# State-space outputs of a hybrid diffusion layer, channel-major: two heads side by side in the array's columns, decays as broadcast rows

## The chip, the cores and the metric

The kernel runs on one core of one Trainium2 chip, in one launch. The metric is device time in microseconds (us). A core has a matrix engine (TensorE, PE in the profile, with its weight loads as PEld), a vector engine (DVE), a scalar engine (ACT), GpSimd (POOL) and SyncE (SP), which issues the DMAs here. SBUF is the on-chip memory of 128 partitions; PSUM holds the results of matmuls.

## The reference, cut to what matters

One layer over 512 latent tokens (and 256 context tokens) of 1024 channels: a modulated norm, one input projection, two token mixers (a state-space scan, "SSD", in both directions, and windowed attention), an output projection, then a gated feed-forward net. The change concerns the outputs of the scan. There are 32 heads of 64 channels in 4 groups of 8; each group has one B and one C of 128 state dimensions; tokens go in chunks of 128.

```python
def ssd_scan(xs, la, bm, cm, h0, with_output):
    ...
    cs = jnp.cumsum(ac, axis=-1)
    ...
    cb = jnp.einsum('bclgn,bcsgn->bgcls', cc, bc)
    scores = cb[:, :, None] * jnp.exp(segsum(ac))
    y_diag = jnp.einsum('bgrcls,bcsgrp->bclgrp', scores, xc)
    y_off = jnp.einsum('bclgn,bcgrpn,bgrcl->bclgrp', cc, states[:, :-1], jnp.exp(cs))
    return (y_diag + y_off).reshape(Bsz, L, G, R, P).astype(xs.dtype), final

def ssd_output(y, xs, z, d_skip, g):
    Bsz, L = y.shape[:2]
    y = y + d_skip.reshape(SSD_GROUPS, SSD_HPG, 1).astype(y.dtype) * xs
    return rmsnorm(y.reshape(Bsz, L, D_SSD) * jax.nn.silu(z), g)
```

The scan runs forward and backward, with its own step sizes dt and decays for each direction, and the two outputs are added. Since x is scaled by dt, the token's own term (l = s) appears in both directions.

## The kernel before, in words

All arithmetic is fp32. The large projections split each operand into a high and a low part and use three matmuls (lines L187, L188, L190; `gemm`), 512 tokens moving, 128 channels at a time. Weights are loaded by SP into `wraw` (3 buffers), split by ACT into `whi` (L144) and by DVE into `wlo` (L145).

After attention, one program list runs the four groups of the scan, with the projections of the next group placed between their steps (in the last group, gate projections `g_step` in their place). A scheduler then sets the order on each engine; every engine, and SP's queue of DMAs, works strictly in its order. `dt_tables` works out dt and the cumulated decays `cs`, writes `cs` to memory (`cs_d`), and `dt_turn` turns the tables token-major: `TA` (biases for the decays), `TB` (exp(cs) of both directions and dt) and `TC`.

For group g:

- `x_fn` projects four tiles of 128 channels, runs the short convolution and silu (L737 to L746) into a scratch tile `tc`, and `turn` transposes it on the PE (L765), so that `xs` is token-major.
- `states` makes the backward states of all chunks and the first forward state (L837, L855; the POOL scales the old state in L839, the DVE adds in L840).
- `chunk_in(c)` fetches `fb`, the decay rows of eight heads copied to all 128 partitions, one tile of 512 KB for each direction (L890, 4 buffers); makes B·C for the chunk (`cb`, L894); takes the diagonal of `cb` with a DVE reduction against the identity (L897) and forms `coef` = dt_b·diagonal + skip weight (L901); and makes `E`, the decayed scores of 4 heads, twice (L909 to L915).
- `chunk_out(c)` makes C·state for both directions (L924, C stationary, 512 columns of state moving), scales each by exp(cs) (DVE, L927), makes the diagonal part head by head (L931: E stationary, 64 columns of `xs` moving), adds `coef`·xs and both off-diagonal parts on the POOL (L936 to L938) and the whole into `y` (DVE, L939), token-major. Then `advance` makes the next forward state.
- `gate` turns `y` back to channel-major with 16 PE transposes (L953), multiplies it by the gate `zs`, fetched from memory (L950, L955), writes it to memory (`yz_d`, L956) and sums its squares (ACT L961, POOL L962).

The sum of squares `ssq` is read by the PE in `rms_sums` (L229), which stands among the first products of the next stage (`os_step`, which reads `yz_d` back through `y_split`, L1000 to L1003).

Of the kernel before, what the change touches and what calls it, by code (L numbers as in the profile page):

```python
# [9 lines left out]
F32 = mybir.dt.float32  # L10
# [8 lines left out]
P = 128  # L19
# [25 lines left out]
def tile_hybrid_layer(  # L45
# [62 lines left out]
    def misb():  # L108
        return bank("mis")
# [104 lines left out]
    ao_d = dpool.tile([8, P, L], F32, name="ao_d")  # L214
    yz_d = dpool.tile([16, P, L], F32, name="yz_d")
    cs_d = dpool.tile([64, L], F32, name="cs_d")
    tt_d = dpool.tile([64, 4], F32, name="tt_d")

    def col(base, i):
# [401 lines left out]
    TB = tabp.tile([P, 4, P], F32, name="TB")  # L621
    TC = tabp.tile([P, 4, 64], F32, name="TC")
    eT = tabp.tile([P, 64, 4], F32, name="eT")
    epool = ExitStack()
# [5 lines left out]
    def dt_tables(w):  # L630
# [61 lines left out]
        F["dt"] = sa, sb  # L692
        dump("dt", dt)
        dump("cs", cs)

    def dt_turn():
        sa, sb = F["dt"]
# [71 lines left out]
    def proj_steps(g):  # L769
        d = GR[g]  # L770

        def b_fn(w):
            d["xs"] = bp.tile([P, 4, 512], F32, tag="xs", name="xs", bufs=2)
            d["xsc"] = bp.tile([P, 2, 512], F32, tag="xsc", name="xsc", bufs=1)
            d["Bkc"] = bp.tile([P, 2, P], F32, tag="Bkc", name="Bkc", bufs=2)
# [19 lines left out]
        def x_fn(ct, w):  # L795
            i = 4 * g + ct
            pl, pc = accb(), accb()
            gemm([LAT(pl)], w)
            turn()
            gemm([CTX(pc)], w)  # L800
            for pp, n, dst in ((pl, L, d["xs"]), (pc, LC, d["xsc"])):
                xl = tmp("tc")
# [16 lines left out]
    def ssd_steps(g):  # L819
# [25 lines left out]
        def states():  # L845
# [35 lines left out]
            d["y"] = bp.tile([P, 4, 512], F32, tag="y", name="y", bufs=1)  # L881

        def chunk_in(c):
            fb = []
            for dr in range(2):
                f = bp.tile([P, 8, P], F32, tag="fb", name="fb", bufs=4)
                a = bass.AP(
                    tensor=cs_d.tensor, offset=cs_d.offset + (32 * dr + 8 * g) * L + c * P, ap=[[0, P], [L, 8], [1, P]]
                )
# [5 lines left out]
            cbd = bp.tile([P, 1], F32, tag="cbd", name="cbd", bufs=2)  # L895
            junk = bp.tile([P, P], F32, tag="junk", name="junk", bufs=1)
            V.tensor_tensor_reduce(  # L897
                junk, cb[:, :P], ident, op0=ALU.mult, op1=ALU.add, scale=1.0, scalar=0.0, accum_out=cbd
            )
            coef = bp.tile([P, 8], F32, tag="coef", name="coef", bufs=2)  # L900
            V.scalar_tensor_tensor(coef, TB[:, c, 96 + 8 * g : 104 + 8 * g], cbd, bcs[:, 8 * g : 8 * g + 8], ALU.mult, ALU.add)  # L901
            d["E"], d["coef"] = [], coef
            for q in range(2):
                E = bp.tile([P, 4, P], F32, tag="E", name="E", bufs=3)
                eb = misb()
# [10 lines left out]
                d["E"].append(E)  # L916

        def chunk_out(c):
            xs, y, coef = d["xs"], d["y"], d["coef"]
            tok = slice(c * P, (c + 1) * P)  # L920
            parts = []
            for dr, s in ((0, d["Sf"]), (1, d["Sb"][c])):
                ps = misb()
                T.matmul(ps, d["CT"][:, tok], s, start=True, stop=True)  # L924
                z0 = 32 * dr + 8 * g
                t = tmp("te")
                V.tensor_tensor(h8(t), h8(ps), bc64(TB[:, c, z0 : z0 + 8]), ALU.mult)  # L927
                parts.append(t)
            yd = misb()
            for h in range(8):  # L930
                T.matmul(  # L931
                    yd[:, h * 64 : (h + 1) * 64], d["E"][h // 4][:, h % 4, :], xs[:, c, h * 64 : (h + 1) * 64],
                    start=True, stop=True,
                )
            dx = bp.tile([P, 512], F32, tag="tf", name="dx", bufs=1)
            G.tensor_tensor(h8(dx), h8(xs[:, c, :]), bc64(coef), ALU.mult)  # L936
            G.tensor_tensor(dx, dx, parts[1], ALU.add)
            G.tensor_tensor(dx, dx, parts[0], ALU.add)  # L938
            V.tensor_tensor(y[:, c, :], yd, dx, ALU.add)  # L939
            if c < 3:  # L940
                d["Sf"] = advance(d["Sf"], 0, c, weigh_in(0, c))

        def gate():
            y = d["y"]
            if g == 0:
                dump("y", y[:, 1, :])
            for ct in range(4):
                i = 4 * g + ct
                zt = bp.tile([P, L], F32, tag="zs", name="zs", bufs=2)
                nc.sync.dma_start(zt, zs_d[i])  # L950
                ps = misb()
                for c in range(4):
                    T.transpose(ps[:, c * P : (c + 1) * P], y[:, c, ct * P : (ct + 1) * P], ident)  # L953
                yz = bp.tile([P, 512], F32, tag="tg", name="yz", bufs=2)
                V.tensor_tensor(yz, ps, zt, ALU.mult)  # L955
                nc.sync.dma_start(yz_d[i], yz)  # L956
                if i == 0:
                    S.activation(ssq, yz, AF.Square)
                else:
                    sq = bp.tile([P, 512], F32, tag="th", name="sq", bufs=1)  # L960
                    S.activation(sq, yz, AF.Square)  # L961
                    G.tensor_tensor(ssq, ssq, sq, ALU.add)  # L962

        r = [([], states)]
        for c in range(4):
# [406 lines left out]
```

## Time and profile before

| | us |
|---|---|
| median of 3 runs | 1318.2 (1317.3 to 1318.23) |
| the profiled execution | 1317.22 |
| its span | 1315.4 |
| PE busy / weight loads busy | 1270.1 / 1028.7 |
| DVE / ACT / POOL busy | 912.7 / 640.5 / 133.3 |

The span is what the profile covers of the execution; 1.8 us lie around it. The four groups of the scan lie between about 466 and 792 us. Matmuls are pipelined, so one matmul's duration overlaps the next one's; the time between starts, or a merged row of many, tells what one costs the PE. An fp32 matmul that is not split by hand appears as two records (x2).

### The profile page before, as it was taken

To read this page: it belongs to the slowest core of one execution; us is meant where nothing else is said; L and a number is where in the kernel's file an instruction comes from. 1 tells how busy PE (TensorE), PEld (TensorE's weight loads), DVE (VectorE), ACT (ScalarE), POOL (GpSimd) and SP (SyncE) were. 2 spreads that over 40 slices of the span, in tenths; PEclk is the share of its full clock that TensorE was granted. 3 is DMA by queue.
4 is the path that set the end of the run, shared out by engine and by line. 5 is a ranking of instruction groups with operands and counts; after the bars stand their busy time and mean duration, and the time that the engine had idled before them with its cause. 6 is when DMAs were issued, how large, how long until landed. Compare 5 with 4: busy or idle time off the path is not lost.

```text
span 1315.4 us, 17187 instructions
## 1 busy us (share of the span) xinstructions
PE 1270.1 (97%) x6434; PEld 1028.7 (78%) x6434; DVE 912.7 (69%) x1457; ACT 640.5 (49%) x1182; POOL 133.3 (10%) x104
## 2 busy tenths in 40 slices
PE   4989999999999999999999999999999999999996
PEld 2777777787778878778787787888888888888886
DVE  4578887888666588888888756776677767773333
ACT  4376666666535456475574654223444444442221
POOL 0000000000000024333443430000000000000000
PEclk8998999999999999999999999999999999999998
DMA  7612222211236235444455658767133433333331
GB/s 287 234 33 80 73 80 65 79 67 57 88 112 186 95 93 135 158 112 129 145 123 190 168 166 280 248 204 249 41 116 115 131 104 114 117 110 93 99 89 65
DMA packets 86931, 168.65 MB, mean 128 GB/s; under 512 B 6784, under 2 KB 42112, under 8 KB 86848
## 3 DMA queue, kind: packets, MB, share of 16 engines
q1 hardware_dynamic: 86848, 167.56, 40.9%
q8 instruction: 50, 0.82, 0.3%
q14 instruction: 33, 0.27, 0.1%
HBM read 150.62 MB, written 16.91 MB: 127 GB/s over the span
## 4 chain that ended last, share of the span: by engine, by line
PE 87%; DVE 6%; ACT 3%; issue 1%; DMA 1%; SPq 0%; POOL 0%; DVEq 0%; ACTq 0%; POOLq 0%
PE acc L187 21%; PE acc L188 21%; PE acc L190 21%; PE score L560 2%; PE pt L584 2%; PE mis L924 2%; PE mis L931 2%; PE mis L837 2%; PE po L589 2%; DVE wlo L145 1%; PE po L590 1%; PE mis L855 1%; ACT ta L485 1%; PE mis L765 1%; PE acc L332 1%
## 5 line engine op out<-in xcount | busy, mean ns | idle before, releaser
L145 DVE TENSOR_TENSOR wlo<-wraw,whi 128x1024 fp32r<-128x1024 f32 (+1 forms) x163 | 206.1, 1265 | 133.7 <-ACT whi L144 131.5
L144 ACT CAST whi<-wraw 128x1024 fp32r<-128x1024 f32 (+1 forms) x163 | 168.9, 1037 | 230.5 <-PE acc L188 199.2
L187 PE MATMUL acc<-hlh,whi 128*128 128x512 f32 (+1 forms) x512 | 212.0, 414 | 0.4 <-ACT whi L144 0.4
L190 PE MATMUL acc<-hlh,wlo 128*128 128x512 f32 (+1 forms) x512 | 203.3, 397 | 2.2 <-DVE wlo L145 2.2
L188 PE MATMUL acc<-hll,whi 128*128 128x512 f32 (+1 forms) x512 | 203.5, 398 | 0.0
L187 PE MATMUL acc<-mh,whi 128*128 128x512 f32 x384 | 149.6, 390 | 0.0
L190 PE MATMUL acc<-mh,wlo 128*128 128x512 f32 x384 | 149.4, 389 | 0.0
L188 PE MATMUL acc<-ml,whi 128*128 128x512 f32 x384 | 149.4, 389 | 0.0
L187 PEld LDWEIGHTS acc<-hlh,whi 128*128 128x128 f32 (+1 forms) x512 | 96.7, 189 | 22.1 <-issue 4.1
L190 PEld LDWEIGHTS acc<-hlh,wlo 128*128 128x128 f32 (+1 forms) x512 | 96.3, 188 | 22.1 <-DVE wlo L145 2.9
L188 PEld LDWEIGHTS acc<-hll,whi 128*128 128x128 f32 (+1 forms) x512 | 96.7, 189 | 20.4 <-issue 4.1
L190 PEld LDWEIGHTS acc<-mh,wlo 128*128 128x128 f32 x384 | 72.1, 188 | 15.1
L187 PEld LDWEIGHTS acc<-mh,whi 128*128 128x128 f32 x384 | 72.1, 188 | 15.0
L188 PEld LDWEIGHTS acc<-ml,whi 128*128 128x128 f32 x384 | 72.1, 188 | 14.7
L839 POOL TENSOR_TENSOR st<-st,eT 128x512 f32<-128x512 f32 x24 | 32.8, 1368 | 458.0 <-ACT st L857 444.6
L737 ACT ACTIVATE ta<-acc,half 128x512 f32<-128x512 f32 (+1 forms) x66 | 46.6, 706 | 41.0 <-PE acc L190 41.0
L567 DVE CUSTOM_DVE_ANT_0 p<-score,winm,nsink 128x512 f32<-128x512 f32 (+1 forms) x64 | 52.0, 813 | 18.8 <-PE score L560 17.3
L571 ACT ACTIVATE p<-p,mneg 128x512 f32<-128x512 f32 (+1 forms) x64 | 49.9, 779 | 31.2 <-DVE mneg L567 31.0
L238 POOL TENSOR_TENSOR rs<-ms,phalf 128x2 f32<-128x2 f32 (+1 forms) x7 | 5.5, 790 | 541.0 <-DVE ms L237 541.0
L187 PE MATMUL acc<-fh,whi 128*128 128x512 f32 x154 | 60.0, 390 | 0.0
L190 PE MATMUL acc<-fh,wlo 128*128 128x512 f32 x154 | 59.9, 389 | 0.0
L188 PE MATMUL acc<-fl,whi 128*128 128x512 f32 x154 | 59.9, 389 | 0.0
(309 smaller groups left out, 2766.1 us busy)
## 6 DMA issues: line engine op xcount, KB each, us to landing
wraw<-wup SPq DMA_DIRECT2D x44, 512.0 KB, 3.5
fb<-cs_d SPq DMA_DIRECT2D x32, 512.0 KB, 6.7
wraw<-wm SPq DMA_DIRECT2D x32, 512.0 KB, 3.7
wraw<-wx SPq DMA_DIRECT2D x24, 512.0 KB, 3.6
wm<-wm SPq DMA_DIRECT2D x16, 512.0 KB, 5.5
wraw<-wz SPq DMA_DIRECT2D x16, 512.0 KB, 3.5
wraw<-wg SPq DMA_DIRECT2D x16, 512.0 KB, 3.6
wraw<-wos SPq DMA_DIRECT2D x16, 512.0 KB, 4.7
```

The source lines that it names most:

```text
L144: S.copy(hi[:, :n], r[:, :n])
L145: V.tensor_tensor(lo[:, :n], r[:, :n], raw(hi[:, :n]), ALU.subtract)
L187: T.matmul(ps, wh, xh[:, k0 + k, :], start=a, stop=False)
L188: T.matmul(ps, wh, xl[:, k0 + k, :], start=False, stop=False)
L190: T.matmul(ps, wl, xh[:, k0 + k, :], start=False, stop=b)
L560: T.matmul(ps[:, o : o + w], Q[h][:, b * P : (b + 1) * P], k[:, j, z[0] * P : z[0] * P + w], start=v == 0 and o % 512 in (0, P), stop=v == ...
L567: V.tensor_tensor_reduce(p[:, :n], ps[:, o0 : o0 + n], m, op0=ALU.add, op1=ALU.min, scale=1.0, scalar=nsink[:, h : h + 1], accum_out=mn,)
L571: S.activation(p[:, :n], p[:, :n], AF.Exp, bias=mn, scale=-1.0, accum_out=den[:, i : i + 1])
L584: T.transpose(pt[:, i * P : (i + 1) * P], pts[i][:, c * P : (c + 1) * P], ident)
L589: T.matmul(po, vst[:, t, j, :], pth, start=c == 0, stop=False)
L737: S.activation(o[:, :n], ps[:, :n], AF.Identity, scale=hcol(base_w, stride + i), bias=hcol(base_b, i))
L839: G.tensor_tensor(h8(n), h8(s), bc64(eT[:, z0 : z0 + 8, c]), ALU.mult)
```

## The change

The outputs are made channel-major. A head's 64 channels become the stationary side (64 columns of `xs`) and E moves, 128 tokens wide; the even head of a pair writes PSUM partitions 0 to 63 and the odd one 64 to 127. In C·state, the state is now stationary, 128 columns (two heads) at a time, and C moves: eight matmuls of 128 columns for two of 512. So `y` comes out as channels by tokens, and `gate` needs no transposes. The x tile before its transposition is kept (`xT`, 2 buffers) for the skip term, and `y` is written over it.

The factors that were columns become rows: exp(cs) of both directions and dt_b are written to memory once (`sb_d`, 6 DMAs), and each chunk fetches them as `R` (one buffer of 3 x 4 x 128 numbers a partition), copied to 64 partitions in each of two DMAs of 384 KB. `R` is worked on in place: the POOL multiplies its third part by `cbb`, adds the skip weight `Dc`, multiplies by x, adds the two off-diagonal parts, and the DVE's sum into `y` reads it last. The diagonal of `cb` is made once per group for all tokens: the POOL multiplies C by B, a matmul with ones sums over the state and copies to all partitions (`cbb`). `TB` and its transposes, the DVE's reduction and `coef` go. `fb` has 3 buffers for 4, `Bkc` 1 for 2, and the squares in `gate` are written over `zs`.

```diff
@@ dt_tables, dt_turn @@
+        for u in range(2):
+            for j, r in enumerate((0, 32, 96)):
+                nc.sync.dma_start(sb_d[:, u, j], sb[r + u : r + 32 : 2, :])
+            z = slice(64 * u, 64 * u + 64)
+            G.tensor_copy(Dc[z, :], bcs[z, u:32:2])
...
-        ps = misb()
-        for c in range(4):
-            T.transpose(ps[:, c * P : (c + 1) * P], sb[:, c * P : (c + 1) * P], ident)
-        S.copy(TB.rearrange("p a b -> p (a b)"), ps)
@@ states @@
+                ps = misb()
+                T.matmul(ps, ones, d["cp"], start=True, stop=True)
+                d["cbb"] = bp.tile([P, L], F32, tag="cbb", name="cbb", bufs=1)
+                S.copy(d["cbb"], ps)
...
+            cp_ = tmp("te")
+            G.tensor_tensor(cp_, d["CT"], d["BT"], ALU.mult)
+            d["cp"] = cp_
@@ chunk_in @@
-                f = bp.tile([P, 8, P], F32, tag="fb", name="fb", bufs=4)
+                f = bp.tile([P, 8, P], F32, tag="fb", name="fb", bufs=3)
...
-            V.tensor_tensor_reduce(
-                junk, cb[:, :P], ident, op0=ALU.mult, op1=ALU.add, scale=1.0, scalar=0.0, accum_out=cbd
-            )
-            coef = bp.tile([P, 8], F32, tag="coef", name="coef", bufs=2)
-            V.scalar_tensor_tensor(coef, TB[:, c, 96 + 8 * g : 104 + 8 * g], cbd, bcs[:, 8 * g : 8 * g + 8], ALU.mult, ALU.add)
+            R = d["R"] = bp.tile([P, 3, 4, P], F32, tag="R", name="R", bufs=1)
+            for u in range(2):
+                z = slice(64 * u, 64 * u + 64)
+                a = bass.AP(
+                    tensor=sb_d.tensor, offset=sb_d.offset + (2 * g + u) * 12 * L + c * P, ap=[[0, 64], [L, 12], [1, P]]
+                )
+                nc.sync.dma_start(R[z].rearrange("p a b t -> p (a b) t"), a)
@@ chunk_out @@
-            parts = []
-            for dr, s in ((0, d["Sf"]), (1, d["Sb"][c])):
+            y = d["xT"][:, :, tok]
+            dx = R[:, 2]
+            G.tensor_tensor(dx, dx, d["cbb"][:, tok].unsqueeze(1).to_broadcast([P, 4, P]), ALU.mult)
+            G.tensor_tensor(dx, dx, Dc[:, 4 * g : 4 * g + 4].unsqueeze(2).to_broadcast([P, 4, P]), ALU.add)
+            G.tensor_tensor(dx, dx, y, ALU.mult)
+            for dr, st in ((0, d["Sf"]), (1, d["Sb"][c])):
                 ps = misb()
-                T.matmul(ps, d["CT"][:, tok], s, start=True, stop=True)
-                z0 = 32 * dr + 8 * g
-                t = tmp("te")
-                V.tensor_tensor(h8(t), h8(ps), bc64(TB[:, c, z0 : z0 + 8]), ALU.mult)
-                parts.append(t)
+                for h in range(4):
+                    z = slice(h * P, (h + 1) * P)
+                    T.matmul(ps[:, z], st[:, z], d["CT"][:, tok], start=True, stop=True)
+                V.tensor_tensor(flat(R[:, dr]), ps, flat(R[:, dr]), ALU.mult)
+                G.tensor_tensor(dx, dx, R[:, dr], ALU.add)
             yd = misb()
             for h in range(8):
                 T.matmul(
-                    yd[:, h * 64 : (h + 1) * 64], d["E"][h // 4][:, h % 4, :], xs[:, c, h * 64 : (h + 1) * 64],
-                    start=True, stop=True,
+                    yd[64 * (h % 2) : 64 * (h % 2) + 64, (h // 2) * P : (h // 2 + 1) * P],
+                    xs[:, c, h * 64 : (h + 1) * 64], d["E"][h // 4][:, h % 4, :], start=True, stop=True,
                 )
-            dx = bp.tile([P, 512], F32, tag="tf", name="dx", bufs=1)
-            G.tensor_tensor(h8(dx), h8(xs[:, c, :]), bc64(coef), ALU.mult)
-            G.tensor_tensor(dx, dx, parts[1], ALU.add)
-            G.tensor_tensor(dx, dx, parts[0], ALU.add)
-            V.tensor_tensor(y[:, c, :], yd, dx, ALU.add)
+            V.tensor_tensor(y, yd.rearrange("p (a b) -> p a b", a=4), dx, ALU.add)
@@ gate @@
-                ps = misb()
-                for c in range(4):
-                    T.transpose(ps[:, c * P : (c + 1) * P], y[:, c, ct * P : (ct + 1) * P], ident)
-                yz = bp.tile([P, 512], F32, tag="tg", name="yz", bufs=2)
-                V.tensor_tensor(yz, ps, zt, ALU.mult)
+                yz = d["xT"][:, ct, :]
+                V.tensor_tensor(yz, yz, zt, ALU.mult)
...
-                    sq = bp.tile([P, 512], F32, tag="th", name="sq", bufs=1)
-                    S.activation(sq, yz, AF.Square)
-                    G.tensor_tensor(ssq, ssq, sq, ALU.add)
+                    S.activation(zt, yz, AF.Square)
+                    G.tensor_tensor(ssq, ssq, zt, ALU.add)
```

In the order that results on each engine, the PE's sequence is the old one with these exchanges. On SP, the two DMAs of `R` for chunk c+1 stand behind a wait for the DVE's `y` of chunk c. On the POOL, the three steps on `dx` of a group's first chunk stand ahead of that group's scalings of states, and in the later chunks the scaling of the forward state stands behind the two additions (in one chunk of the last group between them).

More of the change, by code (lines that the diff above doesn't have):

```diff
@@ L216, in tile_hybrid_layer @@
     cs_d = dpool.tile([64, L], F32, name="cs_d")
+    sb_d = dpool.tile([4, 2, 3, 4, L], F32, name="sb_d")
     tt_d = dpool.tile([64, 4], F32, name="tt_d")
@@ L696, in dt_turn @@
     def dt_turn():
-        sa, sb = F["dt"]
+        sa = F["dt"]
         ps = misb()
@@ L774, in b_fn @@
             d["xsc"] = bp.tile([P, 2, 512], F32, tag="xsc", name="xsc", bufs=1)
-            d["Bkc"] = bp.tile([P, 2, P], F32, tag="Bkc", name="Bkc", bufs=2)
+            d["xT"] = bp.tile([P, 4, L], F32, tag="xT", name="xT", bufs=2)
+            d["Bkc"] = bp.tile([P, 2, P], F32, tag="Bkc", name="Bkc", bufs=1)
             d["Bk"] = bp.tile([P, 4, P], F32, tag="Bk", name="Bk", bufs=2)
@@ L801, in x_fn @@
             for pp, n, dst in ((pl, L, d["xs"]), (pc, LC, d["xsc"])):
-                xl = tmp("tc")
+                xl = tmp("tc") if n < L else d["xT"][:, ct, :]
                 conv_silu(pp, n, i, xl)
@@ L894, in chunk_in @@
             T.matmul(cb[:, :P], d["BT"][:, tok], d["CT"][:, tok], start=True, stop=True)
-            cbd = bp.tile([P, 1], F32, tag="cbd", name="cbd", bufs=2)
-            junk = bp.tile([P, P], F32, tag="junk", name="junk", bufs=1)
-            V.tensor_tensor_reduce(
-                junk, cb[:, :P], ident, op0=ALU.mult, op1=ALU.add, scale=1.0, scalar=0.0, accum_out=cbd
-            )
-            coef = bp.tile([P, 8], F32, tag="coef", name="coef", bufs=2)
-            V.scalar_tensor_tensor(coef, TB[:, c, 96 + 8 * g : 104 + 8 * g], cbd, bcs[:, 8 * g : 8 * g + 8], ALU.mult, ALU.add)
-            d["E"], d["coef"] = [], coef
+            R = d["R"] = bp.tile([P, 3, 4, P], F32, tag="R", name="R", bufs=1)
[5 more added lines that the diff above has]
+                nc.sync.dma_start(R[z].rearrange("p a b t -> p (a b) t"), a)
+            d["E"] = []
             for q in range(2):
@@ L918, in chunk_out @@
         def chunk_out(c):
-            xs, y, coef = d["xs"], d["y"], d["coef"]
+            xs, R = d["xs"], d["R"]
             tok = slice(c * P, (c + 1) * P)
-            parts = []
-            for dr, s in ((0, d["Sf"]), (1, d["Sb"][c])):
-                ps = misb()
-                T.matmul(ps, d["CT"][:, tok], s, start=True, stop=True)
-                z0 = 32 * dr + 8 * g
-                t = tmp("te")
-                V.tensor_tensor(h8(t), h8(ps), bc64(TB[:, c, z0 : z0 + 8]), ALU.mult)
-                parts.append(t)
+            y = d["xT"][:, :, tok]
[4 more added lines that the diff above has]
+            for dr, st in ((0, d["Sf"]), (1, d["Sb"][c])):
+                ps = misb()
+                for h in range(4):
[3 more added lines that the diff above has]
+                G.tensor_tensor(dx, dx, R[:, dr], ALU.add)
             yd = misb()
```

8 lines of the change are left out of this document (2 added, 6 removed).

## The prediction

> **What bounds the kernel now.** I read the page's busy times and chain first, then the busy times by stage, then the four groups of the scan instruction by instruction.
>
> ```profile
> span 1315.4 us, 17187 instructions
> PE 1270.1 (97%) x6434; PEld 1028.7 (78%) x6434; DVE 912.7 (69%) x1457; ACT 640.5 (49%) x1182; POOL 133.3 (10%) x104
> PE 87%; DVE 6%; ACT 3%; issue 1%; DMA 1%; SPq 0%; POOL 0%; DVEq 0%; ACTq 0%; POOLq 0%
> ```
>
> ```profile
> 466.00:549.00 83.00, 82.87 (x446) 65.46 (x445) 68.68 (x105) 50.16 (x118) 29.39 (x20) 1.00 0.45 127
> 549.00:631.00 82.00, 81.12 (x442) 64.49 (x440) 68.59 (x103) 49.29 (x116) 31.76 (x22) 1.00 0.47 133
> 631.00:715.00 84.00, 82.77 (x445) 65.59 (x446) 69.87 (x106) 50.33 (x119) 32.09 (x22) 1.00 0.49 139
> 715.00:792.00 77.00, 76.27 (x353) 57.86 (x351) 51.90 (x79) 43.85 (x100) 33.34 (x25) 1.00 0.59 181
> ```
>
> The columns of the second fence are the stretch, its length, the busy times of PE, PEld, DVE, ACT and POOL, the granted clock, the DMA share and GB/s. Each row is a group of the scan. The PE is busy practically all the time at full clock, so work taken off it shortens the stage, as long as nothing else comes up to its pace. The nearest is the DVE, which inside the chunks of a group stands much higher than over the group:
>
> ```profile
> 571.77:584.77 13.00, 13.00 (x73) 10.44 (x73) 11.74 (x20) 10.38 (x28) 4.98 (x4) 1.00 0.59 144
> 584.77:599.15 14.38, 14.38 (x88) 11.92 (x87) 12.36 (x20) 10.38 (x28) 5.69 (x4) 1.00 0.51 130
> 599.15:612.85 13.70, 13.70 (x80) 11.24 (x80) 11.28 (x20) 9.26 (x24) 4.60 (x3) 1.00 0.54 134
> ```
>
> A chunk takes 13.7 us on the mean in the first three groups, of which the DVE works 11.8.
>
> **The PE's account.** These rows of the chain give the prices:
>
> ```profile
> 44.74 1.00 PE acc L332 x16
> 501.90 1.72 PE mis L924 x4
> 503.62 1.73 PE mis L931 x16
> 775.43 1.75 PE mis L953 x16
> ```
>
> Diagonal part (L931): 16 passes a chunk in 1.73 us, 0.108 each, though only 64 columns move: a pass of L924 with 512 columns takes 0.43, so 128 columns take as long as such a pass does now, and the swap alone gains nothing. What can gain is that two heads use different columns of the array. The trace shows this overlap at L332, a product of the opening stage: four lanes of 32 columns, 256 columns moving, 16 passes. By L924's rate they would take 16 x 0.215 = 3.44 us one after the other; they took 1.00. For two lanes I take 0.95 us a chunk, between one half (0.86) and no overlap (1.73): 16 chunks x 0.78 = 12.5 us saved (0 to 13.9).
>
> The Trainium skill, page "TensorEngine Tiling (Array Packing)", section "Key Properties", says that changing the tiling mode drains the array, which speaks against the change, since each chunk goes in and out of it. L332 pays for two such switches within its 1.00 us, 0.14 over the 0.86 of a perfect overlap, so by the trace the rule costs 0.1 us a chunk at most, which is in my 0.95.
>
> Transposes in `gate`: 4 x 1.75 = 7.0 saved. Transposes of TB: four, 0.4. C·state: 16 passes of 128 columns at 0.108 = 1.73 for 1.72, nothing. Added: the matmul with ones, two passes of 512 columns, 4 x 0.86 = 3.4. Sum for the PE: 12.5 + 7.0 + 0.4 - 3.4 = 16.5 us less, 4.1 a group.
>
> **POOL and DVE.** The groups of instructions between 466 and 784 us:
>
> ```profile
> L145 DVE TENSOR_TENSOR wlo<-wraw,whi 128x1024 fp32r<-128x1024 f32 x28 | 43.7, 1561 | 2.6 <-ACT whi L144 2.6
> L938 POOL TENSOR_TENSOR dx<-dx,te 128x512 f32<-128x512 f32 x16 | 26.9, 1679 | 1.3
> L936 POOL TENSOR_TENSOR dx<-xs,coef 128x512 f32<-128x512 f32 x16 | 22.1, 1384 | 28.6 <-DVE coef L901 28.6
> L937 POOL TENSOR_TENSOR dx<-dx,te 128x512 f32<-128x512 f32 x16 | 21.9, 1370 | 109.1 <-DVE te L927 109.1
> L939 DVE TENSOR_TENSOR y<-mis,dx 128x512 f32<-128x512 f32 x16 | 11.0, 688 | 16.7 <-POOL dx L938 16.7
> L897 DVE CUSTOM_DVE_ANT_0 junk<-mis,ident 128x128 f32<-128x128 f32 x16 | 4.5, 283 | 0.0
> L901 DVE SCALAR_TENSOR_TENSOR coef<-TB,cbd,bcs 128x8 f32<-128x8 f32 x16 | 4.5, 281 | 0.1
> ```
>
> POOL: three steps of 4.43 us a chunk become five. Three come ahead of the off-diagonal parts (two like L936, one like L937: 4.14), two after them (L937, L938: 3.05), 7.2 in all. DVE: L897 and L901 go (0.56 a chunk); L927's successor and the gate's product keep their shape and price. Against that stands a collision:
>
> ```profile
> 710.61 2.33 DVE L145 TENSOR_TENSOR wlo<-wraw,whi 128x1024 fp32r<-128x1024 f32 x1
> 710.57 1.30 POOL L962 TENSOR_TENSOR ssq<-ssq,sq 128x512 f32<-128x512 f32 x1 [5.62 <-ACT sq L961]
> 579.60 1.26 DVE L145 TENSOR_TENSOR wlo<-wraw,whi 128x1024 fp32r<-128x1024 f32 x1
> ```
>
> The same split takes 1.26 us while the POOL rests and 2.33 beside a POOL step of 1.30. That is the exclusive lock of the Trainium skill's page "SBUF — State Buffer", section "Who interferes with whom"; the trace agrees. With 2.8 us more POOL work a chunk I estimate 0.6 more on the DVE (a quarter of the steps colliding), which takes back what L897 and L901 gave. So the DVE stays at some 11.8 us a chunk.
>
> **The loop through R.** R has one buffer, and its last reader is the DVE's sum into y. So the fetch for chunk c+1 is queued on SP behind y(c), and y(c+1) follows only after fetch, three POOL steps, two POOL additions and the sum. Before, `fb` with four buffers was fetched a chunk ahead, and L936 needed only `coef`: there was no such loop.
>
> ```profile
> fb<-cs_d SPq DMA_DIRECT2D x32, 512.0 KB, 6.7
> DMA to landing us min/median/max: 5.1/6.7/13.0
> zs<-zs_d SPq DMA_DIRECT2D x16, 256.0 KB, 3.3
> ```
>
> The second row is fb's. R comes as two DMAs of 384 KB, in runs of the same 512 bytes, three quarters of fb's pair; I take 6.8 from the issue of the first to the landing of the second (5.0 if the engines are free, 8.5 if the next fb, queued right behind, shares them). The loop: 6.8 + 4.14 + 3.05 + 0.69 + 0.3 of wakes between six steps = 15.0 us a chunk (13 to 17). The PE would need 13.7 - 0.78 = 12.9 in the first three groups, and in the last, which has no context products, 10.5 - 0.78 = 9.7 (y was spaced 10.5 there, by the rows below). **The loop is longer than the PE's chunk everywhere**, and the DVE, which works in order, holds weight splits and convolutions behind the waits for R and for the POOL.
>
> What does that make of the time? I follow y through a group, in the times of before:
>
> ```profile
> 574.94 0.68 DVE L927 TENSOR_TENSOR te<-mis,TB 128x512 f32<-128x512 f32 x1
> 578.78 0.69 DVE L939 TENSOR_TENSOR y<-mis,dx 128x512 f32<-128x512 f32 x1 [1.19 <-POOL dx L938]
> 620.91 0.68 DVE L939 TENSOR_TENSOR y<-mis,dx 128x512 f32<-128x512 f32 x1
> 737.25 0.68 DVE L927 TENSOR_TENSOR te<-mis,TB 128x512 f32<-128x512 f32 x1
> 741.62 0.69 DVE L939 TENSOR_TENSOR y<-mis,dx 128x512 f32<-128x512 f32 x1 [1.95 <-POOL dx L938]
> 773.20 0.69 DVE L939 TENSOR_TENSOR y<-mis,dx 128x512 f32<-128x512 f32 x1 [2.84 <-POOL dx L938]
> 784.82 1.81 POOL L962 TENSOR_TENSOR ssq<-ssq,sq 128x512 f32<-128x512 f32 x1 [0.82 <-ACT sq L961]
> 789.95 0.95 PE L229 MATMUL mis<-rmsc,ssq 128*128 128x1 f32 x8
> ```
>
> First three groups (the second as example): the first chunk's R is long there, so y(0) follows the second scaling, 575.6 + 1.4 + 0.7 = 577.7. Three loops on, y(3) is at 622.7; before it ended at 621.6. So y comes 1.1 us later, while the PE would have been 4.1 us ahead. The next group's convolutions stand behind y(3) on the DVE, and the PE's transposes (L765) behind those. So these groups give back what the PE saved: I take 0 for the three (each between -4.1 and +3).
>
> Last group: y(0) at 737.9 + 1.4 + 0.7 = 740.0, y(3) at 785.0, where it ended at 773.9. `gate` then takes: two products 1.4, square and POOL addition about 2, a fetch of zs that now waits for that addition, 3.3, two products, square and addition 3.5, in all some 10.5 us (12.7 before, with the transposes). ssq is complete at 795.5. The PE's L229 reads it and stands ahead of the products of the next stage: 795.5 for 789.95, +5.5. Before, ssq was 3.3 us early (786.6), the cover that is now gone. A PE idle for some us also loses its clock:
>
> ```profile
> 97.00:105.00 8.00, 5.34 (x13) 3.74 (x14) 7.74 (x12) 5.60 (x8) 0.00 (x0) 0.50 0.30 97
> ```
>
> for which I add 1.5. Sum: 0 + 5.5 + 1.5 = +7. The profiled execution, 1317.2, lies 1.0 under the median; added to the median that gives **1325 us**.
>
> ```profile
> 581.68 0.63 ACT L914 ACTIVATE E<-E 128x512 f32<-128x512 f32 x1 [2.44 <-DVE E L913]
> ```
>
> At nothing I cost the six small writes of sb_d (the dt stage, weights loaded ahead; at most 2 us if SP's queue makes a weight late) and fb's third buffer: its second half comes one chunk later but still before its ACT steps, behind which ACT idled 2.4 us, by this row; if not, up to 1 us a chunk, in the range.
>
> **The rivals.** *The PE's saving arrives.* R lands in 5 us, as the smallest fb did, the POOL steps take their undisturbed times, and the loop is 13 us: no longer than the PE's chunk in three groups. Then these give 12.3 us, the last group's y(3) is 6 us earlier than above on its own and 12.3 by the shift, and ssq no longer holds the PE up by more than a few us: 1302 to 1310. For it: y before was spaced 14.0 us in the second group (578.78 to 620.91, three steps) with no loss, and the scheduler's order keeps R's fetch ahead of other loads. Against: the median fb.
>
> *A longer loop, from the DMA and the lock.* The DMA share is 0.45 to 0.59 already, R adds 12.6 MB, and fb, weights and R now ask at the same moment, after y. From 16 us on each step of nine loops loses against before as well: at 16.5, 9 x 1.5 + 3 x 1.5 = 18 us more than forecast, 1343.
>
> *The pairs do not overlap.* The alternating halves run one after the other: the PE saves 4.0 instead of 16.5. Where the loop binds, little of this shows, 1327; where it doesn't, 1314.
>
> **How the numbers follow.** The forecast (loop 14.2 to 15.8, 1316 to 1334) 0.46; the PE's saving arrives 0.26; a longer loop 0.20; no overlap 0.08. A measurement can tell about 0.2%, 2.6 us, from no change. Faster: the second case, a quarter of the fourth and the forecast's lower edge, 0.30. The same: 0.09 from the forecast's edge. Slower: 0.61. The range takes in loops from 13.3 to 16.6 us: 1304 to 1345.
>
> **What would show it.** L947 in merged rows of 16 at about 0.95 us; L953's successor gone; y spaced 15 us in all groups, R's landing near 7 us, the DVE idle before R's scaling (waiting for the DMA) and before y (for the POOL); the PE waiting for ssq before its product with rmsc, and for DVE steps ahead of the turns. Wrong, if y is spaced under 13.5 us, if the PE stays at 99% through the groups, or if the time is under 1315.

## The result, and the profile after

The changed kernel takes 1368.1 us (median of 4 runs, 1364.7 to 1370.9) against 1318.2: 1.038 of the time before, 95% interval 1.0354 to 1.0407. It is slower by 50 us, where 7 were forecast and 27 was the end of the range. The profiled execution took 1365.6 us with a span of 1363.5.

The same lines of the page as before, the chain by line, and the row of its DMA part for R (KB of each transfer, median us from issue to landing):

```profile
span 1363.5 us, 17569 instructions
PE 1278.2 (94%) x6566; PEld 1035.9 (76%) x6566; DVE 916.6 (67%) x1409; ACT 642.1 (47%) x1185; POOL 178.1 (13%) x142
PE 64%; DMA 12%; DVE 9%; POOL 7%; ACT 5%; issue 3%; SPq 0%; POOLq 0%; DVEq 0%; ACTq 0%
PE acc L187 16%; PE acc L190 16%; PE acc L188 16%; DMA R<-sb_d 7%; POOL R L943 2%; PE score L561 2%; PE pt L585 2%; DVE wlo L145 2%; POOL R L936 2%; PE po L590 2%; DMA zs<-zs_d 1%; DMA fb<-cs_d 1%; PE po L591 1%; POOL R L934 1%; POOL R L935 1%
R<-sb_d SPq DMA_DIRECT2D x32, 384.0 KB, 5.9
```

The PE carried 87% of the chain that ended last; now it carries 64%, and transfers 12% instead of 1%, most of it the fetch of R. The POOL grew by 44.8 us (178.1 - 133.3) and is still busy only 13% of the time: a chain runs through an engine that is nearly idle.

The start of each sum into y shows where the time went (the DVE's timeline, one group and the last; in brackets the idle time before it and what ended it):

```profile
592.16 0.68 DVE L951 TENSOR_TENSOR xT<-mis,R 128x512 f32<-128x512 f32 x1
608.25 0.69 DVE L951 TENSOR_TENSOR xT<-mis,R 128x512 f32<-128x512 f32 x1 [2.56 <-POOL R L943]
641.66 0.69 DVE L951 TENSOR_TENSOR xT<-mis,R 128x512 f32<-128x512 f32 x1 [2.54 <-POOL R L943]
686.57 0.68 DVE L951 TENSOR_TENSOR xT<-mis,R 128x512 f32<-128x512 f32 x1
774.63 0.69 DVE L951 TENSOR_TENSOR xT<-mis,R 128x512 f32<-128x512 f32 x1 [1.18 <-POOL R L943]
821.50 0.69 DVE L951 TENSOR_TENSOR xT<-mis,R 128x512 f32<-128x512 f32 x1 [5.30 <-POOL R L943]
```

In the second group y(0) to y(3) took 49.5 us for 42.1 before; from y(3) to the next group's y(0), the "gap", 44.9 for 41.9; the last group 46.9 for 31.6. Over the four groups the stretches from y(0) to y(3) grew by 34.9 us and the three gaps by 11.7. The last y begins 48.3 us later than before (821.5 for 773.2), and from there to the end of the span it is 542.0 us for 542.2. So all of the loss lies in the scan. Busy times by stage, cut at these sums (the columns are those of the prediction's second fence), two rows of after and the same two of before:

```profile
592.00:641.70 49.70, 46.65 (x314) 40.03 (x313) 35.53 (x51) 27.81 (x70) 25.26 (x18) 1.00 0.62 165
641.70:686.60 44.90, 37.92 (x179) 27.30 (x178) 34.90 (x45) 23.61 (x52) 19.45 (x14) 0.96 0.48 147
578.80:621.00 42.20, 42.20 (x244) 34.97 (x243) 36.78 (x59) 25.44 (x63) 15.76 (x11) 1.00 0.49 129
621.00:662.80 41.80, 40.91 (x209) 31.03 (x208) 33.24 (x47) 24.71 (x56) 16.22 (x12) 1.00 0.48 143
```

The PE, never idle in these chunks before, now stands still 3 of 49.7 us there and 7 of 44.9 in the gap, and its granted clock was 0.96 in the gap.

One round of the loop, from the chain of waits (start, length, what; the pieces called "issue" left out):

```profile
592.16 0.69 DVE xT L951
...
592.87 0.59 SPq L912
...
593.51 7.65 DMA R<-sb_d
...
601.32 1.29 POOL R L934
...
602.67 1.37 POOL R L935
...
604.12 1.30 POOL R L936
...
605.49 1.36 POOL R L943
...
606.92 1.31 POOL R L943
...
608.25 0.70 DVE xT L951
```

This is the loop that the prediction drew, 16.1 us instead of 15.0: from the end of y to the first POOL step 8.5 us (the forecast had 6.8 for the fetch), the five POOL steps 6.9 (7.2).

### The profile page after: what moved, and what is told of

Read it like the earlier page. It is cut to its first block, busy times and chain, and to the rows that moved or that the text cites. A ratio compares the mean times of both kernels' runs of the same rounds, so it can differ in the third digit from the quotient of the medians.

```text
span 1363.5 us, 17569 instructions
## 1 busy us (share of the span) xinstructions
PE 1278.2 (94%) x6566; PEld 1035.9 (76%) x6566; DVE 916.6 (67%) x1409; ACT 642.1 (47%) x1185; POOL 178.1 (13%) x142
## 4 chain that ended last, share of the span: by engine, by line
PE 64%; DMA 12%; DVE 9%; POOL 7%; ACT 5%; issue 3%; SPq 0%; POOLq 0%; DVEq 0%; ACTq 0%
PE acc L187 16%; PE acc L190 16%; PE acc L188 16%; DMA R<-sb_d 7%; POOL R L943 2%; PE score L561 2%; PE pt L585 2%; DVE wlo L145 2%; POOL R L936 2%; PE po L590 2%; DMA zs<-zs_d 1%; DMA fb<-cs_d 1%; PE po L591 1%; POOL R L934 1%; POOL R L935 1%
## 5 line engine op out<-in xcount | busy, mean ns | idle before, releaser
L190 PE MATMUL acc<-hlh,wlo 128*128 128x512 f32 (+1 forms) x512 | 206.7, 404 | 5.7 <-DVE wlo L145 5.7
L739 ACT ACTIVATE ta<-acc,half 128x512 f32<-128x512 f32 (+1 forms) x66 | 46.6, 706 | 29.9 <-PE acc L190 29.9
L740 DVE SCALAR_TENSOR_TENSOR ta<-acc,half,ta 128x511 f32<-128x511 f32 (+1 forms) x66 | 43.8, 664 | 21.1 <-ACT ta L739 20.8
```

The lines of the kernel that those rows point to most:

```text
L190: T.matmul(ps, wl, xh[:, k0 + k, :], start=False, stop=b)
L739: S.activation(o[:, :n], ps[:, :n], AF.Identity, scale=hcol(base_w, stride + i), bias=hcol(base_b, i))
L740: V.scalar_tensor_tensor(o[:, 1:n], ps[:, 0 : n - 1], hcol(base_w, i), o[:, 1:n], ALU.mult, ALU.add)
```

## The experiments

Times are medians, ratios are to the kernel before on the same chip, with 95% intervals.

**Three buffers for fb, in the kernel before.** `bufs=4` becomes `bufs=3`.

> The kernel before with three fb buffers instead of four, nothing else. Theory 'loop' (the single buffer of R sets the pace of the chunks): the third buffer is a side matter, 1316 to 1324 us, y spaced 14 us in the first three groups as before. Rival 'fb' (fewer fb buffers starve ACT, which waited 18.6 us for fb in the changed kernel): 1335 us or more, with ACT's steps on fb waiting for the DMA some 10 times. Rivals 'crowd' and 'gate' expect 1316 to 1320.

1318.4 us, ratio 1.0003 (0.9994 to 1.0013). The third buffer costs nothing, as the prediction had it.

**One fetch of R a group.**

```diff
-            R = d["R"] = bp.tile([P, 3, 4, P], F32, tag="R", name="R", bufs=1)
-            for u in range(2):
+            if c == 0:
+                d["R"] = bp.tile([P, 3, 4, P], F32, tag="R", name="R", bufs=1)
+            R = d["R"]
+            for u in range(2 if c == 0 else 0):
```

> The changed kernel with R fetched only for the first chunk of each group; the later chunks work on what the chunk before left in the tile, so their factors are wrong ones, while every POOL, DVE and PE instruction stays. Theory 'loop': the fetch, 8.5 of the 16.1 us from y to y, is gone, y is spaced 13 us or less in the first three groups and 10 to 11 in the last, 1305 to 1330 us. Rival 'crowd, engines' (more POOL steps that lock the DVE out): POOL and DVE work is the same, so 1350 us or more. Rival 'crowd, DMA' (12.6 MB more traffic makes fb and weights late): 9.4 MB of it go, so it also falls, to about 1330. Rival 'gate' (squares written over zs hold up the next group): 1355 or more.

1328.6 us, ratio 1.0083 (1.0065 to 1.0100): 39 of the 50 us hang on fetching R in every chunk. Ten remain, which this loop can't explain: from y(0) to y(3) a group now takes 39.8, 40.5, 40.4 and 30.3 us, less than before (42.1, 42.1, 42.2 and 31.6), but the gaps stay as long as in the changed kernel (46.5, 46.6 and 41.3, where before had 40.7, 41.9 and 36.6).

**Squares in a tile of their own.** ACT's squares go to `tmp("te")` instead of `zt`, so that `zs` is free sooner.

> The changed kernel with the squares in a scratch tile of their own, so that zs is free again once y was multiplied by it. Rival 'gate': the wait of the second zs pair for the POOL goes (2 to 5 us between y of a group's last chunk and the next group's states), 1350 to 1358 us. Theory 'loop' alone: 1362 to 1368, since the chunks inside a group stay at 16 us apart. Both 'crowd' theories: 1364 to 1370.

1370.8 us, ratio 1.0392 (1.0368 to 1.0417): no gain.

**R split in two.** The rows for dt go to `Rd`, the exponentials to `R`; the third POOL step and the additions write in y's place, so that no fetch waits for the sum into y.

```diff
-            G.tensor_tensor(dx, dx, y, ALU.mult)
+            G.tensor_tensor(y, dx, y, ALU.mult)
...
-                G.tensor_tensor(dx, dx, R[:, dr], ALU.add)
+                G.tensor_tensor(y, y, R[:, dr], ALU.add)
```

> The changed kernel with R in two tiles of one buffer each and the same size together: dt rows (Rd), fetched again as soon as the POOL's third step has read them, and the two exp(cs) rows, fetched again after the POOL's second addition; the third step and the additions write into y's place, so neither tile waits for y. Same bytes, same instructions but for four DMAs a chunk instead of two. Theory 'loop': what remains of a loop is fetch of 512 KB (6 to 7), scaling (0.7), two additions (2.7), 10 to 11.5 us, under the PE's 12.9, so y is spaced about 13 us in the first three groups and 10.5 to 11.5 in the last; 1308 to 1330 us. Rivals 'crowd, engines' and 'crowd, DMA': the traffic and the steps are all still there, 1350 us or more. Rival 'gate': 1355 or more.

1369.4 us, ratio 1.0391 (1.0369 to 1.0414). Inside a group y is now spaced 12.5 to 16.2 us, 10.2 in the last: the loop through y is cut. But the scheduler put all four chunks' first POOL steps ahead, among the scalings of the states, and their fetches ahead of fb in SP's queue. SP's timeline, and a row of this kernel's waits (total, times, longest):

```profile
490.85 8.29 SPq L917 DMA_DIRECT2D Rd<-sb_d  x3
500.46 1.22 SPq L903 DMA_DIRECT2D fb<-cs_d  x2
...
ACT mis L928 <- DMA fb<-cs_d: 26.8, 5, 7.9
```

Three issues for Rd hold the queue for 8.3 us, and fb, which ACT needs for the next chunk, goes out behind them. The wait had moved into the gaps, which take 54.0, 56.5 and 49.1 us.

**The split with the POOL's steps in order.** The three steps of chunk c+1 are traced behind the additions of chunk c and pinned there (`tc.keep_in_program_order`).

> The kernel with R split into the rows for D and dt (Rd) and the exponentials (R), the sums in y's place, and the three POOL steps of chunk c+1 traced and pinned behind the additions of chunk c. The bytes fetched are the same as in the kernel after. The loop theory (it is the wait of fetch behind y, and of y behind fetch, that costs) expects y spaced 12.5 to 13.7 us in the first three groups, gaps as in the kernel after (45), and about 1328, as with one fetch a group. The rival, that the bytes of R themselves slow fb and the weights, or that SP's queue is blocked in either form, expects 1350 or more.

1347.6 us, ratio 1.0227 (1.0209 to 1.0244). With the same bytes 20 us come back: half of what leaving out the fetches gives. Neither 1328 nor "1350 or more" was right. Nor was the spacing of y: 13.4 to 16.8 us in the first three groups, where 12.5 to 13.7 were expected; 12 of the 20 us come back in the last group. Part of what is left shows among its waits in the first group's chunks (497 to 545 us):

```profile
ACT mis L944 <- DMA fb<-cs_d: 5.6, 1, 5.6
```

fb still goes out behind Rd and R in SP's queue.

**The gate behind the convolutions.** In the kernel after, only the four products of `gate` are pinned behind what was traced on the DVE.

```diff
-                V.tensor_tensor(yz, yz, zt, ALU.mult)
+                m = V.tensor_tensor(yz, yz, zt, ALU.mult)
+                tc.keep_in_program_order(m)
```

The reason is in the gap of the kernel after (chain of waits):

```profile
546.66 1.31 DVE xT L961 x2
...
548.44 5.87 DMA zs<-zs_d
...
554.94 1.22 DVE wlo L145
...
559.05 1.36 DVE tc L748
...
560.54 0.66 PE mis L767 x2
```

Before, the PE's transposes of y kept the gate's products back. Without them they start right after y(3), and the DVE waits for `zs` with the last convolution (L748), for which the PE's turn (L767) waits, behind it.

> The kernel after, with only the four gate products (and so their squares) pinned behind the convolutions of the next group's x(3). The gate theory (without the transposes of y the gate's products are ready at once after y(3), and their squares stand on ACT, and a wait for zs on DVE, ahead of the convolution for which the PE's turns wait) expects each of the three gaps between groups to shrink to what it was before: 45 to 41, 44 to 41, 39 to 36.6, in all 9.5 us: 1358. The rival, that the gaps only look longer since the loop through R has displaced work into them, expects no gain: 1366 to 1372.

1364.6 us, ratio 1.0365 (1.0348 to 1.0382): 3.5 us, not 9.5, and the interval overlaps that of the kernel after (1.0354 to 1.0407), so that a gain isn't shown. Two of the gaps did shrink (46.2, 44.9 and 39.9 became 41.9, 44.0 and 40.5), but y inside the groups took 2.8 us more in all: while the loop stands, it takes back most of what the gate gives.

**Both.** Split in order, and the late gate.

> The split with ordered POOL steps and the gate pinned behind the convolutions. If both theories hold and add, 1328 - 9.5 = 1318, as the kernel before or better, down to 1302 if the PE's saving of 16.5 us then arrives in full. If the gate theory falls, as the split alone; if the loop theory falls, above 1345.

1345.0 us, ratio 1.0209 (1.0194 to 1.0224): 2.6 us less, again with overlapping intervals. The two don't make 1318.

**One fetch, late gate.**

> R fetched for the first chunk of each group only (the decays of the other chunks are then wrong), and the gate pinned. This is the change without its fetches and without the early gate. Gate theory: 1328.6 - 9.5 = 1319. If the PE's saving then arrives in full, 1302. If what was left in the kernel with one fetch came from the POOL's longer chain instead, 1328 stays.

1325.9 us, ratio 1.0066 (1.0051 to 1.0081): again 2.7, within the intervals, and here the last y begins as late as without the pin (781.85 and 781.89), so that the traces put nothing of it into the gaps. The three pairs point the same way, but no one of them shows a gain by itself. What was left showed on the POOL in the gap (timeline):

```profile
551.04 1.74 POOL L936 TENSOR_TENSOR R<-R,cbb 128x512 f32<-128x512 f32 x1
552.86 1.37 POOL L937 TENSOR_TENSOR R<-R,Dc 128x512 f32<-128x512 f32 x1
554.30 1.63 POOL L938 TENSOR_TENSOR R<-R,xT 128x512 f32<-128x512 f32 x1
555.90 1.50 POOL L842 TENSOR_TENSOR st<-st,eT 128x512 f32<-128x512 f32 x1
```

The three steps for chunk 0, which nobody needs for 20 us more, stand ahead of the first scaling of a state (L842), on which the backward states and the PE's products L840 hang.

**One fetch, late gate, first chunk's steps behind the state chain.** The same pin on L936 for c = 0.

> The kernel with one fetch of R a group and the late gate (1325.9), with one thing more: the three POOL steps on the first chunk's R are pinned behind the POOL's products of the state chain (st by eT), ahead of which they stood in the gap. If the POOL's queue in the gap is what holds the state chain, and with it the PE (gaps of 45.8, 45.4 and 42.6 us, where before had 40.7, 41.2 and 36.6), each gap shrinks by about 3 us: 1317. The rival, that collisions of DVE and POOL lengthen the gap whatever the order, expects 1324 to 1328.

1320.2 us, ratio 1.0016 (1.0006 to 1.0026): 5.8 us less, clear of both intervals; 9 were expected. In this kernel, too, the factors of three chunks in four are wrong ones.

**R by the POOL's own queue, in the kernel after.** `nc.sync.dma_start` becomes `nc.gpsimd.dma_start`.

> The kernel after, with R fetched by the POOL's own DMA queue in place of SP's: nothing of SP (fb, weights, zs) waits behind R any more, while y still waits for R and R for y. The loop theory expects y spaced 16 us or more as before the move and 1360 to 1372; if the waits ahead of fb and weights on SP are what costs, 1350 or less. A POOL that pays for the issue of its transfers would make it slower than 1372.

1399.5 us, ratio 1.0607 (1.0570 to 1.0644): slower by 31 us than the change itself. Taking R out of SP's queue does not help while the loop stands, and this queue makes the loop longer (its timeline and chain):

```profile
504.70 2.29 POOL L890 TENSOR_TENSOR te<-CT,BT 128x512 f32<-128x512 f32 x1
506.95 1.52 POOL L912 DMA_DIRECT2D R<-sb_d  x2
...
507.71 10.06 DMA R<-sb_d
```

The two issues take 0.76 us each of the POOL and stand behind a step for the next group, and R has landed 10.1 us after the first issue, for 7.65 in the round of SP's queue shown above. In the rounds that the two chains hold it is 7.1 to 10.4 us for the POOL's queue (nine) and 6.8 to 7.9 for SP's (twelve).

**All measures, with each of three queues.** Split, ordered POOL steps, late gate, late first steps; Rd and R fetched by the POOL's queue, by ACT's (`nc.scalar.dma_start`), and by SP's.

> All measures together: R split into Rd and R, POOL steps in order (the first chunk's behind the state chain), gate behind the convolutions, and both fetched by the POOL's queue, so that fb, weights and zs wait for none of them. If loop, SP's queue, gate and the POOL's order in the gap are all of the loss, the PE sets the pace again: 1302 to 1318. If the issue on the POOL costs it 1 us each (four transfers a chunk), 1320 to 1345.

> The same as with the POOL's queue, but both fetched by ACT's queue: the waits of the two transfers for the POOL then stand ahead of ACT's own steps, which were idle 50 of 100. If ACT has room for these waits: 1302 to 1318. If they hold back the convolutions and E: 1330 to 1360.

> The split with ordered POOL steps, late gate and the first chunk's POOL steps behind the state chain, all fetches on SP's queue: the twin of the kernels with the POOL's and with ACT's queue. The late first steps gave 5.8 us with one fetch a group; if they give the same here, 1345 - 6 = 1339, and the queue (ACT's: 1340) makes no difference. If SP's queue, with fb waiting behind R and Rd, is what is left of the loss, this is 1345 and ACT's queue is worth 5.

POOL's queue 1359.9 (ratio 1.0317, 1.0294 to 1.0339), ACT's 1340.1 (1.0158, 1.0139 to 1.0178), SP's 1339.5 (1.0162, 1.0146 to 1.0178). The POOL's queue is 15 us above the upper figure expected of it. The late first steps again give 5.6 us, clear of the intervals (1345.0 to 1339.5), and SP's queue is no worse than ACT's. So it isn't this queue as such. The Trainium skill, page "DMA: Bandwidth & Descriptors", section "Issuing engines are not separate DMA queues", says that transfers issued by different engines share the same 16 engines, so that another issuer saves issue time alone. SP against ACT agrees (0.6 us apart); the POOL's queue, 20 us slower, does not behave as an equal.

**No R at all, and R's bytes without anyone waiting.** The first takes every factor from `cbb`, which makes them wrong ones; the second adds R's two transfers a chunk, pinned behind the chunk's fb, into a tile that nobody reads.

> The same order of work with no R at all: every factor that came from R is taken from the row C.B already on chip (the decays and dt are wrong), with steps of the same number and size on POOL and DVE. The basis for the next run; all theories expect about 1320, as with one fetch a group and the same order.

> The same without R, plus R's transfers with all their bytes (two of 384 KB a chunk) into a buffer that nobody reads, queued on SP behind each chunk's fb: the traffic without the wait. If what was left after the split is the bytes (sharing the transfer engines with fb and weights), this costs 15 to 20 us over its basis: 1335 to 1340. If it is waits and order, under 5: 1320 to 1325.

1321.4 (ratio 1.0023, 1.0012 to 1.0034) and 1322.7 (1.0034, 1.0023 to 1.0045). The page's traffic of the two:

```profile
DMA packets 87053, 168.87 MB, mean 128 GB/s; under 512 B 6808, under 2 KB 42136, under 8 KB 86968
DMA packets 112142, 181.47 MB, mean 137 GB/s; under 512 B 7320, under 2 KB 67224, under 8 KB 112056
```

The 12.6 MB come back in full and cost 1.3 us, which the intervals don't tell from nothing. Nobody waits for these transfers, though each takes 9.0 us in the median to land, for 5.9 in the kernel after. So R's bytes as such slow nothing here that counts; what R costs in the other versions lies in waiting for it.

**The exponentials made on chip.** ACT makes R from fb (`S.activation(R[z, dr], fb[dr][z, u::2, :], AF.Exp)`, four steps a chunk); only Rd is fetched.

> A version with right values: the exponentials in R (two thirds of its bytes) are not fetched but made by ACT from fb, which has the cumulated sums of all eight heads on every partition; only the rows for dt (Rd, 2 x 128 KB a chunk) are still fetched. Order as in the twin on SP's queue. If R's transfers and waits are the loss, 1320 to 1328. If ACT's four added steps a chunk (some 0.6 us each, 38 us in all) take over, 1335 to 1350.

1364.6 us, ratio 1.0347 (1.0331 to 1.0362), above both ranges expected. By its waits ACT became the long leg (its timeline, and two rows of the waits):

```profile
595.25 2.58 ACT L936 ACTIVATE R<-fb 64x512 f32<-64x512 f32 x4 [1.29 <-POOL xT L965]
...
DVE E L948 <- ACT mis L947: 31.1, 16, 5.8
PE mis L972 <- DVE E L950: 21.3, 7, 5.1
```

The four steps wait for the POOL to free R and hold the steps for E behind them, for which the DVE and then the PE wait.

**fb ahead of R in SP's queue.**

> The twin on SP's queue (1339.5), with the fetches of Rd and R queued behind fb of the same chunk, so that no fb stands behind a transfer that waits for the POOL. There ACT waited 23 us in all for fb, in nine chunks. If that is what remains over the kernel with idle fetches (1322.7), this gives 1323 to 1330. If y still waits for R through the POOL, so that only the place of the wait moves, 1336 to 1342.

1357.9 us, ratio 1.0297 (1.0278 to 1.0316), above both ranges expected. In the kernel with R and Rd ahead (first row), ACT waited for fb; with fb ahead (last two) that wait halves and the POOL waits for Rd:

```profile
ACT mis L944 <- DMA fb<-cs_d: 23.1, 9, 5.3
...
POOL Rd L911 <- DMA Rd<-sb_d: 55.5, 12, 11.4
ACT mis L943 <- DMA fb<-cs_d: 11.6, 6, 2.3
```

The wait only changes its place, and to a worse one. The edit moves more than the order in the queue: Rd is fetched, and its three POOL steps run, within the chunk itself and no longer behind the additions of the chunk before. So it doesn't tell what fb's place alone is worth.

Between the best version that fetches R (1339.5) and the one that doesn't (1321.4) lie 18 us. By the idle fetches it isn't traffic as such; what is left are waits among the fetches of R, Rd and fb, whose buffers (one, one and three) the POOL and ACT free late. How they divide among the three stays open. None of the versions beats the kernel before.

## Why the prediction was wrong

**The direction and the loop were right.** The loop through R exists, sets y's spacing in all four groups, and is longer than the PE's chunk; one fetch a group takes 39 of 50 us away. The size was not right: 48 us of span against 7.

**The PE's account.** The pairs overlap, nearly as forecast. A chunk's 16 passes in the PE's timeline, after and then before, and the groups of instructions of the scan, three of after and three of before:

```profile
601.18 1.09 PE L947 MATMUL mis<-E,xs 128*64 128x128 f32 x16
586.33 1.89 PE L931 MATMUL mis<-xs,E 128*128 128x64 f32 x16
...
L941 PE MATMUL mis<-CT,st 128*128 128x128 f32 x256 | 34.3, 286 | 7.9 <-DVE xT L951 5.5 <-DVE E L924 1.9 <-ACT xs L811 0.5
L947 PE MATMUL mis<-E,xs 128*64 128x128 f32 x256 | 18.9, 282 | 1.3 <-ACT xs L811 1.2 <-DVE E L926 0.2
L870 PE MATMUL mis<-te,ones 128*128 128x512 f32 x8 | 5.0, 710 | 0.0
L924 PE MATMUL mis<-st,CT 128*128 128x512 f32 x64 | 31.0, 598 | 0.0
L931 PE MATMUL mis<-xs,E 128*128 128x64 f32 x256 | 30.9, 271 | 0.0
L953 PE MATMUL mis<-ident,y 128*128 128x128 f32 x64 | 7.6, 272 | 0.0
```

The 1.73 and the 0.95 of the prediction count as the chain does, without the overlap with what ran before; on that scale the passes take 1.02 us (the chain of the kernel with late first steps). 12.0 us are saved on the pairs (forecast 12.5), 7.6 on the transposes (7.0); C·state, costed at nothing, takes 3.3 more, and the product with ones 5.0 instead of 3.4. With the 0.4 of TB that is 11.7 us for 16.5. The rule of the Trainium skill, page "TensorEngine Tiling (Array Packing)", section "Key Properties", that a change of mode drains the array, was put at 0.1 us a chunk. In that chain the 1.02 lies 0.15 above half of 1.73, and the state's product behind the pairs (L840) takes 1.05 us, where L837 took 0.91 behind L931: 0.3 us a chunk at most, some 5 of the 41 us that the forecast missed. The PE's busy time still rose, 1278.2 for 1270.1. Its granted clock was 0.93 to 0.96 in the gaps, where it was 1.00 before; how much of the rise that makes isn't shown.

**POOL and DVE.** That the POOL rose by 2.8 us a chunk, as worked out, is partly luck: the five steps took 109.2 us where the three took 70.9, which is 2.4 a chunk, and the product of C and B (L890), which the sum leaves out, took 6.2 in all. The DVE rose by 3.9 us in all, 0.24 a chunk, where the prediction had it even.

**The loop.** The mis-sized term is the fetch: 6.8 us were taken, from the median of one fb; R is two transfers, issued 0.6 us apart, and from the start of the first issue to the landing of the second it took 8.0 us on the mean of the twelve rounds (7.5 to 8.5; 8.3 in the one shown), nearer to the 8.5 that the prediction gave for when the next fb shares the engines. The five POOL steps took 7.2, as forecast. Over twelve loops 16.1 for 15.0 makes 13 us.

**The first three groups: this step failed.** "So these groups give back what the PE saved: I take 0" let the gaps shrink by what the chunks of these groups grow and a little more, 10.9 us in all: with the last y starting at 784.3 (it ends at 785.0), 784.3 - 495.9 less twelve loops of 15.0 leaves 108.4 for the three gaps, where before had 119.3. They grew, to 131.0: 22.6 us, the largest error. A gap is no slack for the PE to win: it is itself a chain over DVE, ACT and POOL (convolution, turn, weighting, states). Nor did the gaps grow because y(3) came late: with one fetch a group the stretch up to y(3) was shorter than before, and the gaps took 134.4. The change put two things into it to which the prediction gave no price. The first chunk's POOL steps ahead of the states cost 5.6 to 5.8 us in the two kernels in which they were moved. The gate's products, without the transposes that held them back, cost 2.6 to 3.5 by the medians of three pairs of kernels, none of which tells it from nothing. What else lengthens the gaps stays open; the rivals below show one trace of it.

**The last group.** y was spaced 15.6 us for 15.0 forecast. The gate took 11.9 us from the end of y(3) (822.2) to the end of the last addition (834.1, by the POOL's timeline), for 10.5. The prediction let the stage win back 4.1 us behind y(3); it won back 0.2. These rows close the account: loops 13.0, first y late 1.6, gaps 22.6, behind y(3) 3.9, together the 41.1 us between the span forecast (1322.4) and the span measured.

**The rivals.** "The PE's saving arrives" fell, and not only by the loop: without any R the kernel takes 1321, so the 11.7 us saved on the PE never reach the end, even where nothing waits for R. In the kernel with one fetch, late gate and late first steps, y(0) to y(3) is 1.3 to 2.4 us shorter than before in each group (39.8 for 42.1 in the first), and each gap 2.9 to 4.0 longer (the columns as above; before had 40.7 us there, with the PE idle 0.6):

```profile
536.00:579.70 43.70, 40.77 (x212) 30.83 (x211) 34.88 (x45) 23.82 (x53) 18.60 (x13) 1.00 0.55 156
```

The PE arrives earlier and waits 2.9 us for the gap's chain. The POOL's timeline of this gap shows where:

```profile
550.23 1.06 POOL L842 TENSOR_TENSOR st<-st,eT 128x512 f32<-128x512 f32 x1 [1.01 <-ACT st L860]
552.64 3.31 POOL L972 TENSOR_TENSOR ssq<-ssq,zs 128x512 f32<-128x512 f32 x2 [1.35 <-ACT zs L971]
555.92 3.51 POOL L842 TENSOR_TENSOR st<-st,eT 128x512 f32<-128x512 f32 x2
```

Two additions of the gate's squares (L972) stand between the first and the second scaling of a state (L842). The second begins 20.0 us after y(3); before, with all such additions ahead of the first, it began 16.8 us after (554.81 and 538.05). These 3 us are as much as the gap has grown; no run moved the additions, so that they are its cause is not shown.

"A longer loop" was the nearest: 16 us and more, but at 16.5 it gave 1343, since it had the same step with the gaps. "No overlap" fell by the pairs' row. Of the two side costs put at nothing, fb's third buffer was nothing by its run; the writes of sb_d weren't tried by themselves, and the first y came 1.6 us late.

## What to carry to other kernels

A buffer that is fetched only after its last reader, and whose data the next such reader needs, is a loop: add up its whole round, with the landing of its last transfer, and set it against the pace of the bounding engine in every stage; 12.6 MB that nobody waited for cost nothing clear of the noise here, and waiting for them 39 us. A step that is removed from a queue may have been what held the next one back: ask what now runs early, and what that stands in front of. And a saving on the busiest engine counts only where it also sets the pace of the stretch that follows; before it is booked, follow the chain through the stretch where another engine leads.

## What the runs showed of the hardware

Idle transfers of 384 KB, two a chunk, cost 1.3 us in 1321 at a mean of 137 GB/s, no more than the intervals leave open. A transfer issued by the POOL's queue took 0.76 us of the POOL, and the two of a chunk landed within 7.1 to 10.4 us where SP's took 6.8 to 7.9. Four ACT steps on 64 partitions x 512 took 2.58 us, as long apiece (0.64) as the 0.63 of one on 128 x 512. A PE that idled 7 of 44.9 us showed a granted clock of 0.96 over that stretch, one that idled 7.7 of 46.0 us 0.93.
